# The rotary queries of the first head group ahead of its queries and keys in a latent-attention layer

## The chip, the cores and the metric

The kernel runs on one core of one Trainium2 chip. The metric is the time of one execution on the device in microseconds, the median of three runs. A profile is one further execution, recorded instruction by instruction; its span runs from its first to its last instruction.

## The reference

One hybrid decoder layer on 256 tokens of width 2048, all in float32. The input is normalised and multiplied by one wide matrix. Two of its parts are latents of width 512, one for the queries (q_a) and one for keys and values (c_kv). Cut to what the change touches, the layer then does this for 16 heads:

```
q  = rmsnorm(q_a)  @ w_q_b      # per head: 128 columns q_nope, 64 columns q_rope
kv = rmsnorm(c_kv) @ w_kv_b     # per head: 128 columns k_nope, 128 columns v
q_rope = rope(q_rope);  k_rope = rope(k_rope)
scores = q_nope . k_nope + q_rope . k_rope      # causal, scaled, softmax
attn   = (softmax(scores) @ v) * silu(z_mla)
```

A gated short convolution runs beside the attention; both branches are projected, merged by sigmoid gates, projected again, normalised and added to x.

## The kernel before

Every float32 weight is split into a high part in TensorE's fast 32-bit format (ScalarE, L236, tiles `whi`) and a remainder (VectorE, L237, tiles `wlo`), so that three matmuls make one product of nearly full precision. Weights come in units of 128 x 2048 numbers (1024 KB) through three `raw` buffers, and are split in halves of 1024 columns into five `whi` and five `wlo` buffers.

One list, `plan`, fixes the order in which SP loads the units and in which they are split. `take(i)` (L206) hands unit i to its user and first calls `ahead` (L195), which issues loads up to three units ahead and splits one unit ahead. A unit must therefore be used in the order of the plan. The plan's middle part is built from `order` (L122 to L136): for each head the convolution's four quarter units, every fourth head four gate units `z` and a value unit `v`, and in between the units of the next group of two heads, `a` (queries and keys without position, `wqk`, 1024 KB) and `r` (rotary queries, `wqr`, 256 KB). For the first group both stand in the list `first`, with the value unit behind them.

The emission follows the same lists. At head 0, after the four gate quarters (tiles `z`):

```
790          if h == 0:
791              for i in first:
792                  make(*i)
793              channels(h, 0)
```

`make` calls `group_a` (L549), `group_r` (L558) or `group_v` (L571). `group_a` makes the queries `qn` of two heads from the split latent `qa`, then the keys `kn` from `ckv`, each as sixteen matmuls into two accumulators; `group_r` makes `qr` for both heads with eight matmuls into one accumulator and rotates it (`rope`, L444: `rp_a` L447, four `rp_b` L452, a sum L453); `group_v` makes the values `vv` in two accumulators of twelve matmuls each. An accumulator of qn, kn or qr is emptied by `whole` (L382): ScalarE copies one half of it (`half`, L385), VectorE adds that to the other half (L386, into one of two buffers `f`), and the sum is split again (L236, L237).

Accumulators are PSUM banks handed out in turn:

```
217      def bank(name, tag="mm", bufs=4):
...
562          kw = {} if g else {"tag": "cv", "bufs": 2}
```

Four banks serve z, qn, kn, vv; in group 0, qr uses one of the two `cv` banks, which otherwise hold the convolution's accumulators (tiles `cv`). The gate accumulators of z are emptied by a sigmoid (ScalarE, L673) and a multiplication (VectorE, L674).

Matmuls are kept in program order. On the other engines a scheduler orders the instructions from a model of their times when the program is built; where a step is marked to be kept in program order, it stays. Each engine then runs its own list strictly in order and waits on semaphores.

The latents reach their transposed layout through DRAM: SP writes `far_qa` and `far_ckv` (L318, eight DMAs each) and reads each back with one DMA (L482) into `at_f`; `latent_split` (L485) then scales and splits them into `qa` and `ckv` (ScalarE L490, VectorE L492). SP issues these between the loads of the weights. The SP queue's order in this stretch is: the gate units, far_qa, the first unit of `first`, the return of qa, far_ckv, the second unit of `first`, the return of ckv, the value unit, convolution units. GpSimd computes the angles and copies the rotary tables `cos_t` and `sin_t`.

Of the kernel before, what the change touches and what calls it, by code (L numbers as in the profile page):

```python
# [82 lines left out]
def tile_layer(ctx: ExitStack, tc: tile.TileContext, xw, x, pos, pvec, post_g, wc, wz, wcv, wkr, wqk, wqr, wv, cwr, wsq, out):  # L83
# [34 lines left out]
    for h in range(H):  # L118
        g, second = divmod(h, HG)
        if g + 1 < NG:  # L120
            made[h].append(("a" if second else "r", g + 1))
    first = [("a", 0), ("r", 0), ("v", 0)]  # L122
    order = []
    for h in range(H):
        if h % HV == 0:
# [638 lines left out]
    for h in range(H):  # L764
        v, at = divmod(h, HV)
# [317 lines left out]
```

## Time and profile before

| | |
|---|---|
| median of 3 runs | 1036.09 us (1036.0 to 1036.81) |
| profiled execution | 1037.4 us |
| its span | 1035.6 us |
| TensorE busy / VectorE busy / ScalarE busy | 1025.5 / 682.8 / 526.0 us |
| granted TensorE clock, mean | 0.998 |
| DMA traffic, mean | 225 GB/s |

Times in the views are microseconds from the start of the span. In a timeline a row gives start, length, engine, line, operation, tiles and count, and in brackets how long the engine sat idle before it and who released it. Successive instructions of one kind are merged into one row, whose length runs to the end of the last of them. PE is TensorE, PEld its weight loads, DVE VectorE, ACT ScalarE, POOL GpSimd, SP SyncE, which issues most DMAs; a q behind an engine's name is its instruction queue. L88 is the helper through which all matmuls are emitted, so tiles tell more than lines there. In a table of stretches a row gives the stretch, its length, the busy time (and count) of PE, PEld, DVE, ACT and POOL, the granted clock, the busy share of the DMA engines and GB/s. In a row of DMA issues the last two numbers are the size and the time from issue to landing.

### The profile page before, as it was taken

To read this page: it belongs to the slowest core of one execution; us is meant where nothing else is said; L and a number is where in the kernel's file an instruction comes from. 1 tells how busy PE (TensorE), PEld (TensorE's weight loads), DVE (VectorE), ACT (ScalarE), POOL (GpSimd) and SP (SyncE) were. 2 spreads that over 40 slices of the span, in tenths; PEclk is the share of its full clock that TensorE was granted. 3 is DMA by queue.
4 is the path that set the end of the run, shared out by engine and by line. 5 is a ranking of instruction groups with operands and counts; after the bars stand their busy time and mean duration, and the time that the engine had idled before them with its cause. 6 is when DMAs were issued, how large, how long until landed. Compare 5 with 4: busy or idle time off the path is not lost.

```text
span 1035.6 us, 12709 instructions
## 1 busy us (share of the span) xinstructions
PE 1025.5 (99%) x4672; PEld 853.6 (82%) x4672; DVE 682.8 (66%) x958; ACT 526.0 (51%) x731; POOL 179.5 (17%) x343
## 2 busy tenths in 40 slices
PE   9999999999999999999999999999999999999997
PEld 7888888888888888888888888888888888888885
DVE  7579677777787777867877785564465455455562
ACT  6676555555556455564554564344334434443551
POOL 4641321204201242112313120020010001002000
PEclk9999999999999999999999999999999999999999
DMA  8776766568565685757776765565565556558642
GB/s 337 285 261 227 250 202 230 205 214 308 184 244 211 214 296 171 279 198 243 248 248 207 261 232 205 189 224 197 203 208 208 194 203 234 184 191 332 233 167 81
DMA packets 44670, 233.25 MB, mean 225 GB/s; under 512 B 7968, under 2 KB 10656, under 8 KB 21696
## 3 DMA queue, kind: packets, MB, share of 16 engines
q1 hardware_dynamic: 32544, 199.67, 54.7%
q0 software_dynamic: 11632, 29.48, 8.6%
q10 hardware_dynamic: 432, 3.29, 0.8%
q8 instruction: 36, 0.59, 0.2%
q14 instruction: 26, 0.21, 0.1%
HBM read 215.66 MB, written 12.58 MB: 220 GB/s over the span
## 4 chain that ended last, share of the span: by engine, by line
PE 92%; POOL 4%; issue 2%; DVE 2%; ACT 0%; DVEq 0%; POOLq 0%; ACTq 0%
PE cv L88 34%; PE sq L88 34%; PE out L88 8%; PE z L88 6%; PE vv L88 2%; PE kn L88 2%; PE qn L88 2%; PE sc L88 1%; PE qr L88 1%; POOL ta_y L400 1%; PE o L88 1%; POOL ta_r L403 1%; POOL cos_t L437 1%; DVE wlo L237 1%; POOL sin_t L437 1%
## 5 line engine op out<-in xcount | busy, mean ns | idle before, releaser
L237 DVE TENSOR_TENSOR wlo<-raw,whi 128x1024 fp32r<-128x1024 f32 (+1 forms) x370 | 440.7, 1196 | 285.7 <-ACT whi L236 275.4
L236 ACT ACTIVATE whi<-raw 128x1024 fp32r<-128x1024 f32 (+1 forms) x372 | 383.0, 1035 | 406.7 <-PE sq L88 180.4
L88 PE MATMUL cv<-whi,x_both 128*128 128x512 f32 x1024 | 321.1, 389 | 0.0
L88 PEld LDWEIGHTS cv<-whi,x_both 128*128 128x128 f32 x1024 | 192.3, 188 | 39.3
L88 PE MATMUL cv<-wlo,x_both 128*128 128x512 f32 x512 | 199.5, 390 | 0.0
L88 PE MATMUL sq<-whi,x_both 128*128 128x512 f32 x512 | 158.2, 389 | 0.0
L88 PEld LDWEIGHTS sq<-whi,x_both 128*128 128x128 f32 x512 | 96.1, 188 | 19.9
L88 PEld LDWEIGHTS cv<-wlo,x_both 128*128 128x128 f32 x512 | 96.1, 188 | 19.0
L88 PE MATMUL sq<-wlo,x_both 128*128 128x512 f32 x256 | 99.6, 389 | 0.0
L88 PE MATMUL z<-whi,x_both 128*128 128x512 f32 x256 | 79.9, 389 | 0.0
L88 PE MATMUL sq<-whi,cv_both 128*128 128x512 f32 x256 | 79.4, 389 | 0.0
L88 PE MATMUL sq<-whi,at_both 128*128 128x512 f32 x256 | 79.4, 389 | 0.0
L88 PE MATMUL out<-whi,m_both 128*128 128x512 f32 x256 | 79.0, 389 | 0.0
L318 POOL DMA_DIRECT2D far<-sg x32 | 17.5, 553 | 312.9 <-DVE sg L310 238.3
L318 POOL DMA_DIRECT2D far<-via x64 | 35.3, 558 | 185.4 <-DVE via L310 185.4
L88 PEld LDWEIGHTS out<-whi,m_both 128*128 128x128 f32 x256 | 48.0, 188 | 10.1
L88 PEld LDWEIGHTS sq<-whi,cv_both 128*128 128x128 f32 x256 | 48.0, 188 | 10.0
L88 PEld LDWEIGHTS sq<-wlo,x_both 128*128 128x128 f32 x256 | 48.0, 188 | 10.0
L88 PEld LDWEIGHTS sq<-whi,at_both 128*128 128x128 f32 x256 | 48.0, 188 | 10.0
L88 PEld LDWEIGHTS z<-whi,x_both 128*128 128x128 f32 x256 | 48.0, 188 | 10.0
L88 PE MATMUL z<-wlo,x_both 128*128 128x512 f32 x128 | 49.8, 389 | 0.0
L88 PE MATMUL sq<-wlo,at_both 128*128 128x512 f32 x128 | 49.8, 389 | 0.0
(208 smaller groups left out, 1121.4 us busy)
## 6 DMA issues: line engine op xcount, KB each, us to landing
raw<-wsq_dram SPq DMA_DIRECT2D x80, 1024.0 KB, 4.8
raw<-wcv_dram SPq DMA_DIRECT2D x64, 1024.0 KB, 5.7
raw<-wz_dram SPq DMA_DIRECT2D x16, 1024.0 KB, 4.8
raw<-wqk_dram SPq DMA_DIRECT2D x8, 1024.0 KB, 6.1
cw<-cwr_dram POOLq DMA_DIRECT2D x24, 256.0 KB, 5.9
raw<-wc_dram SPq DMA_DIRECT2D x4, 1024.0 KB, 9.8
raw<-wv_dram SPq DMA_DIRECT2D x4, 1024.0 KB, 6.3
far<-via POOLq DMA_DIRECT2D x64, 48.0 KB, 2.6
```

The costliest lines, as they stand in the source:

```text
L88: return tc.keep_in_program_order(nc.tensor.matmul(*a, **kw))
L236: a = nc.scalar.activation(hi, src, AF.Copy)
L237: b = nc.vector.tensor_tensor(lo, src, hi.bitcast(F32), op=ALU.subtract)
L318: tc.keep_in_program_order(queue.dma_start(out=f[i], in_=m))
L400: tc.keep_in_program_order(nc.gpsimd.tensor_scalar(*a, **kw))
L403: tc.keep_in_program_order(nc.gpsimd.tensor_tensor(*a, op=ALU.subtract))
L437: tc.keep_in_program_order(nc.gpsimd.tensor_copy(dst[to, SQ * q : SQ * (q + 1)], src[ti, :]))
```

## The change

The first two entries of `first` are exchanged. The list is read at two places: it sets the order of the units in the plan, hence SP's loads and the splitting, and the order of emission at head 0. In the new program SP loads `wqr` (256 KB) before the return of qa and `wqk` (1024 KB) before the return of ckv, TensorE makes qr before qn and kn, and the scheduler orders ScalarE's and VectorE's instructions anew around them. The later groups keep their order, and no instruction is added or left out.

```diff
@@ -119,7 +119,7 @@
         g, second = divmod(h, HG)
         if g + 1 < NG:
             made[h].append(("a" if second else "r", g + 1))
-    first = [("a", 0), ("r", 0), ("v", 0)]
+    first = [("r", 0), ("a", 0), ("v", 0)]
     order = []
     for h in range(H):
         if h % HV == 0:
```

## The prediction

> **What bounds the kernel now.** I read the page first, then TensorE's waits over the whole run, then the timelines of TensorE and VectorE between 74 and 94 us, the only stretch where the built order of any engine changes.
>
> ```profile
> span 1035.6 us, 12709 instructions
> PE 1025.5 (99%) x4672; PEld 853.6 (82%) x4672; DVE 682.8 (66%) x958; ACT 526.0 (51%) x731; POOL 179.5 (17%) x343
> PE 92%; POOL 4%; issue 2%; DVE 2%; ACT 0%; DVEq 0%; POOLq 0%; ACTq 0%
> ```
>
> TensorE is busy 99% of the span and is 92% of the chain that ended last: a delay of TensorE anywhere adds its whole length to the time, unless later work had slack to give. TensorE's list of waits for the whole run has three rows:
>
> ```profile
> PE idle L88 <- POOL mhalf L256: 1.0, 1, 1.0
> PE qa L88 <- ACT whi L236: 0.9, 1, 0.9
> PE kn L88 <- DVE at_f L674: 0.4, 1, 0.4
> ```
>
> The columns are total, times and longest. After the third there is no idle gap on TensorE at all, so nothing behind it can absorb a shift. This third wait lies exactly where the change is made. TensorE's timeline there (start, length, tile, idle before):
>
> ```profile
> 75.34 1.98 PE L88 MATMUL qn<-qa,whi 128*128 128x512 f32 x8
> ...
> 78.11 1.09 PE L88 MATMUL kn<-ckv,whi 128*128 128x512 f32 x4
> 79.62 1.21 PE L88 MATMUL kn<-ckv,whi 128*128 128x512 f32 x4 [0.42 <-DVE at_f L674]
> ...
> 81.62 1.09 PE L88 MATMUL qr<-qa,whi 128*128 128x512 f32 x4
> ...
> 83.03 0.40 PE L88 MATMUL vv<-whi,ckv 128*128 128x512 f32 x1
> ...
> 85.79 0.39 PE L88 MATMUL vv<-whi,ckv 128*128 128x512 f32 x1
> ...
> 88.51 0.39 PE L88 MATMUL cv<-whi,x_both 128*128 128x512 f32 x1
> ```
>
> The queries qn take 2.77 us (75.34 to 78.11), the keys kn 3.51 (78.11 to 81.62) for sixteen matmuls of the same shapes, so kn's wait costs 0.74, not only the 0.42 of idle shown. The rotary queries qr take 1.41, each of the two value blocks vv 2.76 and 2.72. VectorE is the engine to watch beside it:
>
> ```profile
> 75.00:80.00 5.00, 4.58 (x25) 3.61 (x24) 5.00 (x9) 3.85 (x6) 0.00 (x0) 1.00 0.96 357
> 80.00:85.00 5.00, 5.00 (x29) 4.33 (x28) 5.00 (x9) 3.82 (x9) 0.00 (x0) 1.00 0.77 270
> ```
>
> The third busy number is VectorE: 5.00 of 5.00 us in both stretches, while over the span it is 66%. Here an evacuation is as late as its place in VectorE's queue.
>
> **The change on TensorE.** qr's eight matmuls move from 81.62 to 75.34; their inputs (the split qa) are what qn needed there anyway, and their accumulator is of another pool, the one for cv. Then qn runs 76.75 to 79.52, and kn's second accumulator is wanted four matmuls later, at 79.52 + 0.92 = 80.44 (vv's twelve from 83.03 to 85.79 take 0.23 each). It is free when VectorE has multiplied the second gate block (L674):
>
> ```profile
> 75.51 0.68 DVE L237 TENSOR_TENSOR wlo<-raw,whi 128x512 fp32r<-128x512 f32 x1
> ...
> 77.11 1.21 DVE L237 TENSOR_TENSOR wlo<-raw,whi 128x1024 fp32r<-128x1024 f32 x1
> ...
> 78.87 0.70 DVE L674 SCALAR_TENSOR_TENSOR at_f<-z,r_both,at_f 128x512 f32<-128x512 f32 x1
> 79.50 1.21 DVE L237 TENSOR_TENSOR wlo<-raw,whi 128x1024 fp32r<-128x1024 f32 x1
> ...
> 81.25 1.18 DVE L237 TENSOR_TENSOR wlo<-raw,whi 128x1024 fp32r<-128x1024 f32 x1
> 82.36 0.74 DVE L386 TENSOR_TENSOR f<-qn,half 128x256 f32<-128x256 f32 x2
> 83.02 1.21 DVE L237 TENSOR_TENSOR wlo<-raw,whi 128x1024 fp32r<-128x1024 f32 x1
> 84.15 0.75 DVE L237 TENSOR_TENSOR qn_lo<-f,qn_hi 128x256 fp32r<-128x256 f32 x2
> 84.82 0.74 DVE L386 TENSOR_TENSOR f<-kn,half 128x256 f32<-128x256 f32 x2
> ...
> 88.33 0.43 DVE L447 TENSOR_TENSOR rp_a<-f,cos_t 128x256 f32<-128x256 f32 x1
> 88.78 1.70 DVE L452 TENSOR_TENSOR rp_b<-f,sin_t 32x256 f32<-32x256 f32 x4
> ...
> 92.25 0.41 DVE L453 TENSOR_TENSOR f<-rp_a,rp_b 128x256 f32<-128x256 f32 x1
> 92.58 1.22 DVE L237 TENSOR_TENSOR wlo<-raw,whi 128x1024 fp32r<-128x1024 f32 x1
> ```
>
> That row ends at 79.57. Up to 81.25 VectorE does the same pieces in the new program; only the half-size piece of qr's weights (0.68) is exchanged for a full one and now comes first, so 79.57 stands. The wait of 0.74 is gone, and vv is due at 83.03 - 0.74 = 82.29.
>
> **What is late next.** There are four accumulators in the main pool, taken in turn: vv's first one is that of qn's first head, vv's second that of qn's second head. In the built program vv_0 waits for the addition (L386) that empties qn_0, vv_1 for the one that empties qn_1. Before, these two additions stand side by side at 82.36. The new order of VectorE from 81.25 on is:
>
> ```
> wlo (conv weights, first half) | f<-qr | wlo (second half) | f<-qn_0 | rp_a | rp_b x4
> | wlo (next conv weights) | qn_lo | f<-rp_a,rp_b | f<-qn_1 | vv_lo | qr x2 | qn_lo | f<-kn_0 | f<-kn_1
> ```
>
> I add steps from start to start, as the rows give them: a full wlo 1.11 (81.25 to 82.36) or 1.13 (83.02 to 84.15), one addition of a pair 0.33 (half of 82.36 to 83.02), rp_a 0.45, the four rp_b 1.70, one qn_lo 0.33 (half of 84.15 to 84.82), the sum after the rotation 0.33 (92.25 to 92.58).
>
> f<-qn_0 starts at 81.25 + 1.11 + 0.33 + 1.13 = 83.82 and, at 0.41 long (0.74 - 0.33), ends at 84.23. kn's matmul followed its releaser by 0.05 (79.57 to 79.62), so vv_0 starts at 84.28: 2.0 us of idle TensorE. It would end at 84.28 + 2.76 = 87.04. f<-qn_1 starts at 83.82 + 0.33 + 0.45 + 1.70 + 1.13 + 0.33 + 0.33 = 88.09 and ends at 88.50, so vv_1 starts at 88.55: a second gap of 1.5. That is 88.55 - 85.79 = 2.76 later than before. After its gap kn's group of four took 1.21 instead of 1.09, so I add 0.12 for the refill: **+2.9 us**. The 0.74 gained is already inside this sum. f<-qn_1 could not move up: it writes the one buffer that qn_lo of the first head has to read first.
>
> Behind it nothing waits longer. The next reader of the late pieces is the first score:
>
> ```profile
> 93.95 0.28 PE L88 MATMUL sc<-kn,qn_hi 128*128 128x256 f32 x1
> ```
>
> It would stand at 96.85, and needs the keys' low part. VectorE reaches the end of that at 88.42 + 7 x 0.41 + 0.68 + 1.13 = 93.1 (seven pieces of 256 columns taken like an addition, vv_lo like the half piece, one full wlo). ScalarE's copies for the additions come before VectorE reaches them, and POOL's order is unchanged.
>
> **The moved DMAs.** SP loads qr's 256 KB in front of qn's and kn's 1024 KB, and the returns of the two latents lie between:
>
> ```profile
> 58.46 0.34 SPq L482 DMA_DIRECT2D at_f<-far_qa  x1
> 59.46 5.68 SPq L318 DMA_DIRECT2D far_ckv<-cw  x8
> 65.24 0.38 SPq L154 DMA_DIRECT2D raw<-wqr_dram  x1
> 66.50 0.34 SPq L482 DMA_DIRECT2D at_f<-far_ckv  x1
> raw<-wqk_dram SPq DMA_DIRECT2D x1, 1024.0 KB, 5.3
> at_f<-far_qa SPq DMA_DIRECT2D x1, 512.0 KB, 6.4
> at_f<-far_ckv SPq DMA_DIRECT2D x1, 512.0 KB, 4.2
> ```
>
> Behind 1024 KB a return takes 6.4 us, behind 256 KB 4.2. So qa comes back at 62.7 instead of 64.9; the last far_ckv, which waits for that landing in the built program, goes out 2.2 earlier, and with it the 1024 KB (63.0) and the return of ckv (64.3). That lands at 64.3 + 6.4 = 70.7, as before (66.50 + 4.2). I cost this at nothing. If the eight far_ckv writes are not faster, it lands at 72.9, 2.2 late. What covers that:
>
> ```profile
> 70.68 1.71 ACT L490 ACTIVATE ckv<-at_f,pv 128x256 fp32r<-128x256 f32 x4 [0.88 <-DMA at_f<-far_ckv]
> 72.30 0.62 ACT L236 ACTIVATE whi<-raw 128x512 fp32r<-128x512 f32 x1
> ...
> 75.22 1.05 ACT L236 ACTIVATE whi<-raw 128x1024 fp32r<-128x1024 f32 x1
> ```
>
> From 70.68 ScalarE works without a pause; the values' first piece ends at 76.27 and VectorE takes it up at 77.11. The new order puts a full piece in place of the one of 0.62, 0.44 longer, so 0.40 us of cover is left, and a return 2.2 late pushes all of VectorE's steps by 1.8. The other way, an earlier return gains nothing, since VectorE is full.
>
> **The rivals.**
> *The latents' return is late:* 2.9 + 1.8 = +4.7, 1040.8. For it: the 1024 KB now lie directly ahead of ckv's return. Against: the same bytes in all, and an earlier start. [...]
> *Only the first gap opens:* if VectorE's steps between the two additions took 1.5 us less than their rows, vv_1 would find its accumulator free: 84.28 - 83.03 + 0.12 = +1.4, 1037.5. Against: these durations repeat closely in the rows shown.
> *Faster:* kn's wait goes and both value accumulators are empty in time. That needs f<-qn_0 by 82.24 and f<-qn_1 by 85.0 (82.29 + 2.76 - 0.05), the latter 3.5 us before my sum. Price -0.74: 1035.4. For it: the work and its inputs are the same, and the wait that goes is real. Against: three other pieces stand between the additions in VectorE's order.
> *The clock drops in the gaps:* had the twelve matmuls of vv_1 half the clock, their 2.72 us would double: 2.9 + 2.7 = +5.6, 1041.7. Against is the stretch with the other long wait:
>
> ```profile
> 8.00:12.00 4.00, 3.06 (x14) 2.48 (x14) 3.52 (x8) 3.76 (x8) 0.00 (x0) 1.00 1.02 415
> ```
>
> 0.94 us idle of 4, and the granted clock stays 1.00. [...]
> *The change does nothing* is out: the order of TensorE, VectorE, ScalarE and SP is changed in the built program.
>
> **How the numbers follow.** The profiled execution took 1037.4 (span 1035.6); with +2.9 it would be 1040.3. The median of the runs, 1036.09, lies 1.3 below it; the shift is the same, so I forecast 1036.09 + 2.9 = 1039.0. About 0.2% (2.07 us, up to 1038.16) is what a measurement can tell from no change. Chances: forecast 0.70 (own range 1038.3 to 1039.8, which takes in up to 0.8 from a return less than fully late), late return 0.12, clock 0.03, first gap only 0.09, faster 0.06. Faster is 0.06; same is the first gap only and a little of the forecast's lower edge, 0.11; the rest, 0.83, is slower. The range runs from 1037.9 to 1041.0: it leaves out faster, first gap only and clock, 0.18.
>
> **What would show it.** In the profile after: TensorE's list of waits has vv waiting for VectorE's L386 twice, about 2.0 and 1.5 us, in place of kn's 0.4; f<-qn_0 near 83.8 and f<-qn_1 near 88.1 on VectorE, the four rp_b between them; cv starting near 91.4 instead of 88.51, and every later TensorE row 2.9 later. A start of L490 for ckv after 71.1 would show the late return. No wait of vv would prove me wrong.

## The result and the profile after

The changed kernel takes 1039.69 us (median of 6 runs, 1039.51 to 1040.21) against 1036.28 (6 runs, 1035.94 to 1036.81) for the kernel before: 3.4 us more, a ratio of 1.003 with a 95% interval of 1.002 to 1.004 (2.1 to 4.1 us). The profiled execution took 1039.71, and its page begins and sums up its chain so:

```profile
span 1037.9 us, 12708 instructions
PE 1025.2 (99%) x4672; PEld 853.4 (82%) x4672; DVE 683.6 (66%) x958; ACT 525.8 (51%) x731; POOL 179.5 (17%) x343
PE 91%; POOL 4%; issue 2%; DVE 2%; ACT 0%; DVEq 0%; POOLq 0%; ACTq 0%
```

TensorE is busy as long as before (1025.2 against 1025.5); what was added is idle time. Its list of waits for the whole run:

```profile
PE vv L88 <- DVE f L386: 1.8, 1, 1.8
PE vv L88 <- ACT qr L236: 1.4, 1, 1.4
PE idle L88 <- POOL mhalf L256: 1.0, 1, 1.0
PE qa L88 <- ACT whi L236: 0.9, 1, 0.9
```

The wait of kn has gone and two waits of vv are there. On TensorE's timeline:

```profile
74.90 1.07 PE L88 MATMUL qr<-qa,whi 128*128 128x512 f32 x4
76.28 2.00 PE L88 MATMUL qn<-qa,whi 128*128 128x512 f32 x8
79.07 2.00 PE L88 MATMUL kn<-ckv,whi 128*128 128x512 f32 x8
83.84 0.50 PE L88 MATMUL vv<-whi,ckv 128*128 128x512 f32 x1 [1.81 <-DVE f L386]
88.24 0.47 PE L88 MATMUL vv<-whi,ckv 128*128 128x512 f32 x1 [1.39 <-ACT qr L236]
91.07 0.39 PE L88 MATMUL cv<-whi,x_both 128*128 128x512 f32 x1
96.51 0.28 PE L88 MATMUL sc<-kn,qn_hi 128*128 128x256 f32 x1
```

qr comes first, kn's sixteen matmuls run through, and each accumulator of the values starts late. From cv to the first score it is 5.44 us (91.07 to 96.51), as before (88.51 to 93.95). Right behind that 0.23 us is won back: from the first score of this head to the next it is 0.34 (96.51 to 96.85) instead of 0.57 (93.95 to 94.52), because the rotated qr is ready in time. VectorE's timeline, which says why; the first row, at which its stretch without a pause begins, is the kernel before's, the others are the changed kernel's:

```profile
65.81 0.35 DVE L440 TENSOR_SCALAR sin_t<-sin_t,pv 128x256 f32<-128x256 f32 x1 [3.48 <-POOL sin_t L437]
```

```profile
65.37 0.35 DVE L440 TENSOR_SCALAR sin_t<-sin_t,pv 128x256 f32<-128x256 f32 x1 [3.47 <-POOL sin_t L437]
...
78.41 0.71 DVE L674 SCALAR_TENSOR_TENSOR at_f<-z,r_both,at_f 128x512 f32<-128x512 f32 x1
...
81.91 0.41 DVE L386 TENSOR_TENSOR f<-qr,half 128x256 f32<-128x256 f32 x1
82.24 1.21 DVE L237 TENSOR_TENSOR wlo<-raw,whi 128x1024 fp32r<-128x1024 f32 x1
83.37 0.41 DVE L386 TENSOR_TENSOR f<-qn,half 128x256 f32<-128x256 f32 x1
83.70 0.41 DVE L447 TENSOR_TENSOR rp_a<-f,cos_t 128x256 f32<-128x256 f32 x1
84.13 1.71 DVE L452 TENSOR_TENSOR rp_b<-f,sin_t 32x256 f32<-32x256 f32 x4
85.87 1.23 DVE L237 TENSOR_TENSOR wlo<-raw,whi 128x1024 fp32r<-128x1024 f32 x1
87.01 0.42 DVE L237 TENSOR_TENSOR qn_lo<-f,qn_hi 128x256 fp32r<-128x256 f32 x1
87.34 0.42 DVE L453 TENSOR_TENSOR f<-rp_a,rp_b 128x256 f32<-128x256 f32 x1
87.68 0.42 DVE L386 TENSOR_TENSOR f<-qn,half 128x256 f32<-128x256 f32 x1
```

The additions that empty the two accumulators stand 4.31 us apart with the rotation between them, and each wait of vv ends just behind one: the addition of 83.37 ends at 83.78 and vv starts at 83.84; that of 87.68 ends at 88.10 and vv starts at 88.24. The list of waits puts the second one down to ScalarE's qr. That is the step which happened to end last. In the third experiment the addition moves up and the wait goes with it, although qr's split comes later there (88.03 instead of 87.80).

Absolute times of two executions don't compare well here, since VectorE's start at L440 moves by some tenths (65.81 and 65.37). Counted from it, the first cv matmul comes 22.70 us after it in the kernel before and 25.70 in the changed one: **+3.0 us**. The two profiled executions as wholes differ by only 2.3 us (1037.4 and 1039.71), since VectorE began 0.44 earlier in the second and the way from the first cv matmul to the end is 0.25 shorter there. The loads:

```profile
69.98 1.71 ACT L490 ACTIVATE ckv<-at_f,pv 128x256 fp32r<-128x256 f32 x4 [0.42 <-DMA at_f<-far_ckv]
64.69 0.34 SPq L482 DMA_DIRECT2D at_f<-far_ckv  x1
```

The return of ckv goes out 1.8 us earlier (64.69 against 66.50) and is used at 69.98 against 70.68: the 1024 KB ahead of it cost nothing in this execution.

### The profile page after: what moved, and what is told of

It is laid out like the page before. It is cut to its first block, busy times and chain, and to the rows that moved or that the text cites. A ratio compares the mean times of both kernels' runs of the same rounds, so it can differ in the third digit from the quotient of the medians.

```text
span 1037.9 us, 12708 instructions
## 1 busy us (share of the span) xinstructions
PE 1025.2 (99%) x4672; PEld 853.4 (82%) x4672; DVE 683.6 (66%) x958; ACT 525.8 (51%) x731; POOL 179.5 (17%) x343
## 4 chain that ended last, share of the span: by engine, by line
PE 91%; POOL 4%; issue 2%; DVE 2%; ACT 0%; DVEq 0%; POOLq 0%; ACTq 0%
PE cv L88 34%; PE sq L88 34%; PE out L88 8%; PE z L88 6%; PE qn L88 2%; PE kn L88 2%; PE vv L88 2%; PE sc L88 1%; PE qr L88 1%; PE o L88 1%; POOL ta_y L400 1%; POOL ta_r L403 1%; DVE wlo L237 1%; POOL cos_t L437 1%; POOL sin_t L437 1%
```

## The experiments

Each kernel is compared with runs of the kernel before on the same chip (medians 1036.52 for experiments 1 to 4, 1036.41 for 5 to 8, 1036.42 for 9 and 10).

**1. Order of computing alone**, and **2. order of loading alone.** The plan (loads and splitting) and the emission are given different orders.

```diff
 e1:
-    first = [("r", 0), ("a", 0), ("v", 0)]
+    first = [("a", 0), ("r", 0), ("v", 0)]
...
-            for i in first:
+            for i in (first[1], first[0], first[2]):
 e2:
-            for i in first:
+            for i in (first[1], first[0], first[2]):
```

> The units are loaded and split in the old order (1024 KB, then 256 KB); only the matmuls, the evacuation and the rotation of qr go ahead of qn and kn. Theory (vv's two accumulators are emptied late, because the rotation stands between the two additions on VectorE): about +3.0 us against the kernel before, the same as the full change (2.5 to 3.6), with two waits of vv for VectorE of about 1.8 and 1.4 us and none of kn. Rival (the moved loads and the latents' returns cost the time): within 0.7 us of the kernel before, and no wait of vv.

> The units are loaded and split in the new order (256 KB, then 1024 KB); the matmuls keep the old order qn, kn, qr, vv. Theory (accumulators): no cost from the loads, within 0.5 us of the kernel before; kn still waits 0.4 us for the second gate block, vv does not wait. Rival (loads and latents' returns): +3 us.

Computing alone: 1039.42, ratio 1.0025 (1.0015 to 1.0034). Loading alone: 1036.45, ratio 0.9998 (0.9990 to 1.0007). TensorE's waits, of the first and of the second:

```profile
PE vv L88 <- DVE f L386: 2.4, 1, 2.4
PE vv L88 <- ACT qr L236: 1.4, 1, 1.4
```

```profile
PE kn L88 <- DVE at_f L674: 0.9, 1, 0.9
```

Both waits of vv come with the order of computing, and so does the time; the moved DMAs cost nothing that these runs can tell.

**3. A third place for the sum.** qr's sum, and its rotated form, go into a free part of `at_f`, so that f<-qn of the second head need not wait for qn_lo of the first.

```diff
-            f = temp("f")
+            f = temp("f") if dst is None else dst
...
-        (f,) = narrow([f"qr{g}"], take(u_grp["r", g]), 0, qa, **kw)
+        (f,) = narrow([f"qr{g}"], take(u_grp["r", g]), 0, qa, None if g else at_f[:, 10, :], **kw)
```

> The full change, but the sum of qr's two halves gets a place of its own instead of one of the two buffers f, so that the sum of the second head of qn need not wait for the first head's split. Built, VectorE then has the addition of qn's second head right behind the four rp_b, one full split, one qn_lo and the rotated sum earlier (1.13 + 0.33 + 0.33 = 1.8 us). Theory: the second wait of vv (1.4 us) goes, the first (1.8) stays: +1.2 to +1.8 us against the kernel before. Rival (one late stream behind both waits, so that the second wait is only made up elsewhere): still +3 us, with the wait moved to the first score or the convolution.

Median 1039.19, ratio 1.0022 (1.0014 to 1.0031), but in two groups: five executions from 1037.71 to 1038.11, seven from 1038.96 to 1041.19. The profiled one took 1037.96. TensorE's waits around the change are down to one:

```profile
PE vv L88 <- DVE f L386: 1.8, 1, 1.8
```

and the timelines of VectorE and TensorE have

```profile
85.77 0.43 DVE L386 TENSOR_TENSOR f<-qn,half 128x256 f32<-128x256 f32 x1
89.32 0.39 PE L88 MATMUL cv<-whi,x_both 128*128 128x512 f32 x1
```

The second addition stands at 85.77 instead of 87.68, directly behind the four rp_b, and the second wait is gone. Its L440 starts at 65.27, so cv comes 24.05 after it: +1.35, the price of the first wait alone. That holds for the lower group; the upper one had another cause.

**4. Other banks for the values.** The first group's two accumulators of vv are taken from the pools of the scores and outputs, which are empty then.

```diff
-            ps = bank(f"vv{v}_{t}")
+            kw = {} if v else {"tag": ("o", "st")[t], "bufs": 1}
+            ps = bank(f"vv{v}_{t}", **kw)
```

> The full change, but the first group's two value accumulators take the two idle banks of the outputs and the scores (tags o and st) instead of those of qn. Theory: neither wait of vv is left, TensorE reaches the first score 3.2 us earlier than with the full change; VectorE, in the order built, ends the keys' low part of the first head only about 0.9 us after TensorE wants it, so the first score waits about 0.9 us. Sum against the kernel before: kn's wait gone (-0.74), the score's wait +0.9: +0.2 us (-0.7 to +0.8). Rival (TensorE's loss does not come from these banks): still about +3 us.

1037.41, ratio 1.0004 (0.9996 to 1.0013). No wait of vv is left, which shows that banks, not data, made vv wait; yet it is not faster than the kernel before. The profiled execution took 1038.31; TensorE's waits around the change:

```profile
PE sc L88 <- DVE kn L237: 1.8, 1, 1.8
PE kn L88 <- DVE at_f L675: 0.5, 1, 0.5
```

The longer one on the timeline:

```profile
95.00 0.39 PE L88 MATMUL sc<-kn,qn_hi 128*128 128x256 f32 x1 [1.76 <-DVE kn L237]
```

The idle time is now in front of the first score, which needs the split keys: VectorE has the same work to do up to there. The profile fell on the slowest of the eleven executions: ckv came late (used at 71.72, 6.83 after L440) and f<-qn_0 stood 19.50 after L440 instead of 18.00, so that kn waited again and the score's wait is longer than the 0.9 that was expected. The medians differ by 0.9, and the interval of the ratio includes 1.

**5 and 6. The change, and the third place, once more** on another chip, for a second profile of each.

> The full change once more, beside the others on one chip. Theory (two late accumulators): two waits of vv, the second ending with VectorE's addition for the second head of qn; between VectorE's start on the rotary tables (L440) and the first convolution matmul 25.7 us against 22.7 in the kernel before, so +3.0 us (2.6 to 3.6). Rival (part of the shift of the medians comes from elsewhere, for instance from late latents): +3.4 us or more, with VectorE waiting for ScalarE ahead of the second L674.

> The full change with a place of its own for qr's sum, once more, since its first times fell into two groups (1037.7 to 1038.1 and 1039 to 1041). Theory (first wait only, +1.3 us, and in some executions the latents' return is late and pushes VectorE by 1 to 2 us): the same two groups; a profile of the slower group would show VectorE waiting for ScalarE ahead of L674. Rival (the second wait is only made up elsewhere): no execution under +2.4 us.

The change: 1039.58, ratio 1.0033 (1.0020 to 1.0045). The third place: 1039.83, ratio 1.0029 (1.0019 to 1.0039), one execution at 1037.10 and seven from 1039.15. Both profiles fell on executions of another kind. Of the changed kernel (1040.75), from the timelines, ScalarE's step on ckv, VectorE's first multiplication of the gates, and TensorE's start of vv and of cv:

```profile
71.74 1.71 ACT L490 ACTIVATE ckv<-at_f,pv 128x256 fp32r<-128x256 f32 x4 [0.81 <-DMA at_f<-far_ckv]
76.74 0.75 DVE L674 SCALAR_TENSOR_TENSOR at_f<-z,r_both,at_f 128x512 f32<-128x512 f32 x1 [0.71 <-ACT at_f L673]
84.89 0.50 PE L88 MATMUL vv<-whi,ckv 128*128 128x512 f32 x1 [2.52 <-DVE f L386]
92.11 0.39 PE L88 MATMUL cv<-whi,x_both 128*128 128x512 f32 x1
```

Its table of stretches (the last three numbers of a row are the granted clock, the DMA share and GB/s):

```profile
85.20:85.60 0.40, 0.40 (x3) 0.33 (x2) 0.39 (x1) 0.35 (x2) 0.00 (x0) 0.80 0.66 271
85.60:86.00 0.40, 0.40 (x3) 0.31 (x2) 0.40 (x1) 0.00 (x0) 0.00 (x0) 0.50 1.10 195
...
88.40:88.80 0.40, 0.40 (x2) 0.33 (x1) 0.40 (x3) 0.00 (x0) 0.00 (x0) 0.50 0.00 0
88.80:89.20 0.40, 0.40 (x3) 0.19 (x1) 0.34 (x2) 0.00 (x0) 0.00 (x0) 0.93 0.00 0
```

Here ckv's return is late, VectorE waits 0.71 for ScalarE ahead of the first L674 and 0.19 behind it, kn waits 0.21 again, the first gap of vv grows to 2.52, and from 85.44 to 88.86 TensorE is granted half its clock. vv's first accumulator runs slowly through the time in which the second would have waited anyway, so the list has no second wait of vv. TensorE did not wait for the late end of that accumulator, but VectorE did, behind its second addition:

```profile
90.17 0.69 DVE L237 TENSOR_TENSOR vv_lo<-vv,vv_hi 128x512 fp32r<-128x512 f32 x1 [1.02 <-ACT vv_hi L236]
```

The first cv matmul comes 26.79 after L440 (65.32), 1.1 later than in the other profile: that is the rival of experiment 5's expectation, except that VectorE waits ahead of the first L674 and not of the second, and VectorE's delay accounts for it (f<-qn_0 at 19.09 after L440 instead of 18.00). Of the third place (1040.0), VectorE's first multiplication of the gates, TensorE's timeline and then the table of stretches:

```profile
76.25 0.75 DVE L674 SCALAR_TENSOR_TENSOR at_f<-z,r_both,at_f 128x512 f32<-128x512 f32 x1 [0.73 <-ACT at_f L673]
84.39 0.80 PE L88 MATMUL vv<-whi,ckv 128*128 128x512 f32 x1 [2.52 <-DVE f L386]
91.33 0.39 PE L88 MATMUL cv<-whi,x_both 128*128 128x512 f32 x1
```

```profile
83.60:84.00 0.40, 0.00 (x0) 0.00 (x0) 0.40 (x2) 0.40 (x1) 0.00 (x0) 0.86 0.97 410
84.00:84.40 0.40, 0.01 (x1) 0.01 (x1) 0.40 (x3) 0.32 (x2) 0.00 (x0) 0.50 1.06 451
...
86.80:87.20 0.40, 0.40 (x3) 0.31 (x2) 0.40 (x2) 0.32 (x1) 0.00 (x0) 0.50 0.00 0
87.20:87.60 0.40, 0.40 (x3) 0.36 (x2) 0.40 (x1) 0.37 (x2) 0.00 (x0) 0.87 0.00 0
```

With no second wait behind it the half clock costs: from the start of vv to cv it is 6.94 us (84.39 to 91.33), in the profile of the lower group 5.57 (83.75 to 89.32), so 1.4 more. It is not all: ckv was late here too, as expected for the slower group, and f<-qn_0 stands 19.11 after L440 (64.81) instead of 18.00. Of the 2.5 us by which cv comes later after L440 than in the lower group (26.52 against 24.05), 1.1 are VectorE's delay and 1.4 the half clock.

**7. The third place with the old loads**, that is experiment 3's diff on experiment 1's kernel, to see whether the upper group comes from the 1024 KB ahead of ckv's return.

> A place of its own for qr's sum and the new order of the matmuls, but the units loaded in the old order, so that 256 KB and not 1024 KB lie ahead of the return of ckv. Theory: first wait of vv only, +1.3 us; and if the slower group of the run with the new loads comes from the 1024 KB ahead of that return, there is no slower group here (all within 1037.2 to 1038.3). Rival (the slower group has another cause): two groups again.

1039.36, ratio 1.0026 (1.0015 to 1.0038): again two groups, three executions from 1037.46 to 1037.68 and four from 1039.36 to 1040.57. The order of the loads is not their cause. The profiled execution (1037.68) is of the lower group and shows one wait and full clock; cv comes 24.06 after L440 (64.98), as in experiment 3:

```profile
83.46 0.50 PE L88 MATMUL vv<-whi,ckv 128*128 128x512 f32 x1 [1.72 <-DVE f L386]
```

**8. The kernel before without kn's wait.** Its keys of the first group go to the empty banks of scores and outputs.

```diff
-            for j, f in enumerate(narrow([f"{n}{g}_{j}" for j in range(HG)], w, HG * (n == "kn"), src)):
+            kws = [{"tag": t, "bufs": 1} for t in ("o", "st")] if g == 0 and n == "kn" else None
+            for j, f in enumerate(narrow([f"{n}{g}_{j}" for j in range(HG)], w, HG * (n == "kn"), src, kws)):
```

> The kernel before, but the first group's two key accumulators take the idle banks of the outputs and the scores, so that kn waits for no gate block. Theory (VectorE, busy without a gap from its start on the rotary tables, sets the time up to the first score, and TensorE's waits only show where it catches up with it): the wait of 0.4 us leaves kn and comes back at the first score, which needs the rotated qr, that VectorE ends at 94.2: no gain, within 0.3 us of the kernel before. Rival (kn's wait is TensorE's own and costs 0.74): -0.7 us, no wait at the score.

1036.92, ratio 1.0005 (0.9996 to 1.0014): taking away the one wait that the change was to remove gains nothing. Its TensorE timeline at the first score, and the same matmul in the kernel before:

```profile
93.97 0.39 PE L88 MATMUL sc<-kr,qr 128*128 128x256 f32 x1 [1.42 <-DVE qr L237]
```

```profile
94.30 0.38 PE L88 MATMUL sc<-kr,qr 128*128 128x256 f32 x1
93.83 0.87 DVE L237 TENSOR_TENSOR qr<-f,qr 64x256 fp32r<-64x256 f32 x2
```

The idle time moves to the score's rotary part. In the kernel before that matmul already starts as the first of the two splits of qr ends (93.83 + 0.87 / 2 = 94.27), 0.23 behind the matmul ahead of it (94.07), where the changed kernel needs 0.06 (96.62 to 96.68): VectorE has nothing to spare there and holds TensorE up by some 0.2 us, which no list of idle time shows.

**9 and 10. The first wait filled with work**, in the kernel with the third place and in the changed kernel.

```diff
             for i in first:
+                if i[0] == "v":
+                    fill = bank("fill", tag="st", bufs=1)
+                    for _ in range(8):
+                        matmul(fill[:, :2 * S], x_both[:, 0, :P], x_both[:, 0, :], start=True, stop=True)
                 make(*i)
```

> The kernel with the third buffer f, and in TensorE's wait ahead of the values' first product (vv) eight matmuls of 128x512 on values that are there already, into a bank that nothing reads before the first score clears it: 8 x 0.23 = 1.84 us of work in place of idle time, in a gap that was 1.8 to 2.5 us long. Theory (the slower executions of the kernel with the third buffer are those in which the gap reached 2.5 us and the granted clock fell to half for some 3 us behind it): nothing that the gap waited for comes sooner, yet the slower group is gone: all executions between 1037.0 and 1038.9, median 1037.9, 1.4 over the kernel before, no stretch of 0.50 in the granted clock, mean clock 0.998. Rival (the spread comes from the latents' return alone, which the matmuls don't touch): two groups as before, median 1039.4.

> The changed kernel with the same eight matmuls in the first of its two waits. Theory: the first chunk of the values then runs at full clock in every execution, but its second accumulator still waits for VectorE's third addition, so that the halved clock that the matmuls prevent had cost little here: median 1039.3, between 1038.9 and 1039.7 (2.9 over the kernel before), with no stretch of 0.50. Rival (the halved clock cost in the changed kernel what it costs with the third buffer, 1.4 us in over half of its executions): median 1038.3 or less, 2.0 over the kernel before.

The third place: 1038.16, ratio 1.0015 (1.0006 to 1.0024); ten of eleven executions lie between 1037.17 and 1038.82, one at 1039.85. Without the filling 18 of 27 executions of experiments 3, 6 and 7 were above 1038.9. The changed kernel: 1039.68, ratio 1.0036 (1.0022 to 1.0049), as without. TensorE's waits around the change, of the one and of the other:

```profile
PE vv L88 <- DVE f L386: 0.4, 1, 0.4
```

```profile
PE vv L88 <- ACT qr L236: 1.4, 1, 1.4
```

Between 78 and 92 us every stretch of both has a granted clock of 1.00; the changed kernel's row with the second wait in it:

```profile
86.00:88.00 2.00, 0.80 (x4) 0.34 (x2) 2.00 (x4) 0.25 (x1) 0.00 (x0) 1.00 0.00 0
```

With the filling the upper group is gone but for one execution, and in the changed kernel the half clock costs nothing that five executions can tell, because the second wait takes it up. Two things limit this. The gaps that these two profiles would have had without the filling are 2.2 and 1.8 us, not 2.5, so the stretches at full clock alone don't show that the filling prevents a fall. The mean clocks say more: none of the 16 filled executions has 0.996, against 13 of the 27 without the filling and 8 of 11 of the changed kernel. And experiments 9 and 10 ran on another chip than 3, 6 and 7; the third place was not run there without the filling. The filling leaves VectorE's delay by late latents as it is, so up to 1.1 us of spread would remain.

## Why the prediction was right, and where not

**kn's wait goes.** Right: L674 ends at 79.12, and kn's second accumulator is due at 79.07 + 0.92 = 79.99. With ckv late the margin is used up, and kn waited 0.21 in experiment 5. But the prediction read 0.74 as TensorE's to win. Experiment 8 shows that it was not: without that wait TensorE stands before the first score for VectorE. The rival *faster* had no way to its -0.74; even with both value accumulators free in time (experiment 4) the kernel stayed at 1.0004.

**The two waits of vv.** Right in cause and place. Counted from L440 the sum put f<-qn_0 at 18.01 (83.82 - 65.81) and f<-qn_1 at 22.28; they came at 18.00 and 22.31. Adding steps start to start, from rows of the same shapes in VectorE's built order, was good to 0.03 us over nine steps. The gaps of the list, 1.81 and 1.39, look smaller than the 2.0 and 1.5 of the sum only because they are counted otherwise: the list counts from the end of the last matmul, the sum from the time at which the next one was due, some 0.16 earlier. Counted like the sum they are 83.84 - (79.07 + 2.79) = 1.98 (kn taken as long as qn, 76.28 to 79.07) and 88.24 - (86.47 + 0.23) = 1.54.

**The sum.** +2.9 forecast, +3.0 from L440 to cv in the profile, +3.4 (2.1 to 4.1) in the medians. The forecast took the shift to be the same for the profiled execution and for the median, and that was not so: the profiled executions differ by 2.3 only. The one of the kernel before lies 1.1 above the median of 1036.28, and VectorE's start at L440 (65.81) is the latest of all twelve profiles, the others having 64.39 to 65.37. The sum also left out the 0.25 that is won behind cv, which goes the other way. The excess of 0.4 of the medians over +3.0 is within the interval. The late return would account for it: the executions profiled show +3.0 with ckv in time and +4.1 with it late, and a mixture lies between. How often it is late is not known, so this is argued, not shown.

**The buffer that holds f<-qn_1 back.** Right: with a third place the second addition moved up by 1.9 us and the second wait went (experiment 3). The price of the rival *only the first gap*, +1.4, is what the lower group and experiment 9 showed (+1.35 from L440, +1.6 with 0.6 to 2.5).

**The moved DMAs at nothing.** Right on the whole (experiment 2). The two returns did not quite exchange their times: that of qa took 4.9 us and that of ckv 5.3, where the forecast had 4.2 and 6.4. The cover of 0.40 us was right too, counted from L440: in the kernel before ckv is used 4.87 after it (70.68 - 65.81), in experiment 5 6.42 (71.74 - 65.32), so 1.55 later, of which 0.40 are covered; the 1.15 left fit the 1.09 by which f<-qn_0 was late. But the return varies between executions under either order of the loads (71.11 with the old one in experiment 1, 69.98 and 71.74 in two of the changed kernel); the change does not make it late, it leaves less cover.

**The clock.** This step failed. The argument was a stretch of 4 us with 0.94 idle at a clock of 1.00; the sum took the gaps of 2.0 and 1.5 at full clock, and the rival had a chance of 0.03. In the profile after the clock stayed at 1.00 through both. But the late return and the clock were priced as two separate rivals, while in experiment 5 they came together: with the latents late the first gap was 2.52, and the clock fell to half. A fall seems to be the usual case: the mean granted clock is 0.996 in four of the changed kernel's first six executions and in four of the five of experiment 5. Of the twelve profiled executions only the two with a fall ahead of vv have 0.996, the others 0.997 to 0.999, and of the 68 of the kernel before beside the experiments two have it (1038.64 and 1039.27 us). For the executions without a profile the fall is an inference from this mean. The profile before has a fall too, at its end: the last matmul ends at 1027.9, the clock falls to half (0.50) at 1032.4 and stays there to the end of the span at 1035.6, 3.2 us; the profile after has 2.9 us of it at its end. The prediction did not use it. That the time came out right all the same was luck as far as the clock goes: the four executions at 0.996 took 1039.51 to 1040.21, the two at 0.999 1039.67 and 1039.71, because the second wait takes up what the half clock costs. The rival's price was wrong as well: it doubled vv's second accumulator, while the half clock falls on the first, whose end TensorE does not wait for.

## What to carry to other kernels

When an operation is moved ahead on the busiest engine, follow what it queues on the engine that empties accumulators: here eight matmuls that cost nothing by their move put a rotation between two evacuations, and the next user of those banks paid for it. A wait removed from an engine at 99% is a gain only if the engine that it waited for is not due again soon; look for the next operand from the same engine that arrives with nothing to spare. Price an idle gap on TensorE also with what the granted clock may do in it or behind it (half for 3.4 us at a gap of 2.52 us in two profiles here, no fall at one of 2.44 in a third), and ask whether a later wait absorbs that.

## What was not expected of the hardware

In two profiles with a gap of 2.52 us without matmuls TensorE's clock was halved for 3.4 us: from 85.44 to 88.86 in experiment 5, from 83.89 to 87.30 in experiment 6 (worked out from the stretches at either end: a clock of 0.86 in 83.60 to 84.00 is 0.11 us at half, so the fall is at 83.89), at a cost of 1.4 us where no later wait took it up. With a gap of 2.44 in experiment 1 the clock stayed at 1.00 in every stretch from 70 to 100 us, and so it did with the gaps of 1.7 to 1.8 that were profiled (the changed kernel, experiments 3, 4 and 7). The fall came at different points, 3.1 us after the gap began in experiment 5, 0.55 after work had resumed, and 2.0 us after it began in experiment 6, inside the gap. TensorE worked 0.9 us and 1.4 us of the 3.4 us ahead of the two falls, so it was idle for 2.5 and 2.0 of them. In experiment 1 a stretch of 3.4 us around the gap had 2.44 idle, more than the 2.0 of experiment 6, and no fall followed. So idle time in the 3.4 us before does not decide it alone, and what does was not shown.

The kernels before and after also have a fall behind their last matmul, which ends at 1027.94 and 1030.27: the clock falls to half at 1032.39 and 1035.02, 4.45 and 4.75 us later.
